# Mixture-of-experts kernel: gate and up as one product of 512 columns, the down projection as three float32r products, one accumulator, other weight rings

## The chip, the cores and the metric

The kernel runs on one core of a Trainium2 chip. The metric is the device time of one launch in microseconds (us). Five compute queues work side by side: TensorE (PE, matrix products; PEld is its weight loading), VectorE (DVE), ScalarE (ACT), GpSimd (POOL) and SyncE (SP, which here only issues transfers). Sixteen DMA engines move the data. Each queue runs its own instructions in order and waits on semaphores for the others.

## The reference

One block of a diffusion backbone: 512 tokens of width 1024 pass a token mixer (retention and gated delta rule) and then a mixture of experts. The change concerns the second half:

```
scores = sigmoid(xt @ w_router)                      # 512 tokens x 64 experts
sel    = 8 experts a token, from the best 4 of 8 groups
wts    = scores[sel] / sum * 2.5
yb     = (silu(xe @ w_gate[e]) * (xe @ w_up[e])) @ w_down[e]     # e = 0..63
routed = sum over the chosen experts of wts * yb
x      = x + g2 * rmsnorm(routed + shared) * norm_ffn_post
```

Each expert has w_gate and w_up of 1024x256 and w_down of 256x1024, all float32: 1 MB each, 3 MB an expert, 192 MB in all. The output must agree with a float32 computation.

## The kernel before, in words

The token mixer takes the first 700 us or so. Then phaseM walks over 64 experts, one block of 128 token slots for each, and a 65th block, "extra", for an expert with more than 128 tokens (its weights are fetched by an indirect load, L1191; a runtime loop at L1459 would handle further ones and runs zero times here).

For each expert e, in the loop at L1424:

- SP loads the three weight matrices into raw buffers (`load`, L1193). Gate and up share six buffers (`GU`), down has three (`DW`); a buffer is reloaded for expert e+3 as soon as it has been consumed.
- `convert` splits a gate or up matrix into two float32r matrices whose sum is the float32 value: ACT casts the high part (L1171, 2048 columns), DVE subtracts to get the low part (L1173). The down matrix stays float32.
- POOL gathers the 128 token rows (L1228); PE turns them (L1236), ACT and DVE split them into high and low (L1238, L1239).
- `proj` multiplies by gate and then by up. Each of 8 row blocks is three products, high x high, high x low, low x high (`mm3`, L111 to L113), 256 columns wide.
- `act` is silu(gate) times up (ACT L1248, DVE L1249), `turn_act` turns the result (L1256, L1258), and `down` multiplies by the float32 down matrix (L1267; four matrix products of 512 columns, each carried out in two passes, so eight instructions in the trace), scales the two halves (DVE L1271, ACT L1269) and adds the rows into a DRAM accumulator with an indirect DMA that adds (L1272, "the scatter").

There are two accumulators, `accd[0]` and `accd[1]`, used in turn (the last blocks all use 1). Scatters into the same accumulator wait for each other. After the loop both accumulators are read back (L1476), added (L1478), normalised (L1481 and the power on POOL at L127), scaled (L1484) and added to x (L1486, L1488).

The order of the instructions on each engine is set by a scheduler that takes the program's order and the dependencies; a buffer ring's depth therefore decides how far one queue runs ahead of another. On SP a load stands behind every load issued before it.

Of the kernel before, what the change touches and what calls it, by code (L numbers as in the profile page):

```python
# [19 lines left out]
D = 1024  # L20
# [3 lines left out]
NE = 64  # L24
# [47 lines left out]
class K:  # L72
# [128 lines left out]
    def run(self, upto="end"):  # L201
        nc, tc, a = self.nc, self.tc, self.a
        main = self.main = self.pool("main")
        self.pes = ExitStack()
        self.psum = self.pool("ps", es=self.pes, space=PSUM)
        self.wi = a["w_in"][0].rearrange("(k p) n -> p k n", p=128)
        self.ident = main.tile([128, 128], F32, name="ident")
        self.mhalf = main.tile([128, 1], F32, name="mhalf")
        nc.vector.memset(self.mhalf, -0.5)
        self.eps = main.tile([128, 1], F32, name="eps")  # L210
        nc.vector.memset(self.eps, EPS)
        self.vecT = main.tile([128, 68], F32, name="vecT")
# [3 lines left out]
        self.w8 = {"a": self.pool("w8a", bufs=4)}  # L216
# [768 lines left out]
    def phaseO(self):  # L985
# [7 lines left out]
        self.accd = [dp.tile([512, 1024], F32, name=f"acc{i}") for i in range(2)]  # L993
# [79 lines left out]
        def shared_down(t):  # L1073
            y = self.rawp.tile([128, 1024], F32, name="y", tag="raw")
            for c in range(2):
                ps = self.pa()
                for k in range(2):
                    nc.tensor.matmul(ps, sgs[t][:, k * 128:k * 128 + 128], wsh[2][:, k, c * 512:c * 512 + 512], start=k == 0, stop=k == 1)  # L1078
                nc.scalar.copy(y[:, c * 512:c * 512 + 512], ps)
            nc.scalar.dma_start(self.accd[0][t * 128:t * 128 + 128], y)  # L1080
# [77 lines left out]
    def phaseM(self):  # L1158
# [7 lines left out]
        T8 = lambda name: self.wt8([128, 2048], F32R, name, "b")  # L1166

        def conv(w, eng, n):
            h, l = T8("wh"), T8("wl")
            for i in range(0, 2048, max(n, 1024)):  # L1170
                nc.scalar.copy(h[:, i:i + max(n, 1024)], w[:, i:i + max(n, 1024)])  # L1171
            for i in range(0, 2048, n):
                eng(l[:, i:i + n], w[:, i:i + n], h[:, i:i + n].bitcast(F32), op=OP.subtract)  # L1173
            return h, l


        hx = self.hxpool.tile([128, 2, 2048], F32, name="wgu", tag="b0")
        GU = [self.wt8([128, 2048], F32, "w", "a") for _ in range(4)] + [hx[:, 0], hx[:, 1]]
        wd2 = q.tile([128, 2, 2048], F32, name="wd", bufs=1)
        DW = [wd2[:, 0], wd2[:, 1], self.keep.tile([128, 2048], F32, name="wd", tag="k0")]  # L1180
        NAMES3 = ("w_gate", "w_up", "w_down")
        wf = {n: a[n][0].rearrange("e (p k) f -> (e p) (k f)", p=128) for n in NAMES3}
        raw = lambda e, n: DW[e % 3] if n == 2 else GU[(2 * e + n) % 6]
# [11 lines left out]
        for e, n in ((0, 0), (0, 1), (1, 0), (0, 2), (1, 1), (2, 0), (1, 2), (2, 1), (2, 2)):  # L1195
            load(e, n)
# [22 lines left out]
        xg6, xg3 = q.tile([128, 3, 1088], F32, name="xg", bufs=1), self.hxpool.tile([128, 3, 1088], F32, name="xg", tag="b1")  # L1219
        xgs = [x[:, i] for x in (xg6, xg3) for i in range(3)]  # L1220
# [4 lines left out]
        def gather(ix):  # L1225
            xg = xgs[ng[0] % 6]
# [14 lines left out]
        def proj(out, x, w, first=True):  # L1241
            for k in range(8):
                s = slice(k * 256, k * 256 + 256)
                self.mm3(out, x[0][:, k], x[1][:, k], w[0][:, s], w[1][:, s], k == 0, k == 7)
# [7 lines left out]
        def turn_act(sg):  # L1252
# [4 lines left out]
            aT = q.tile([128, 256], F32, name="aT")  # L1257
            nc.scalar.copy(aT, ps[:, 0:256])  # L1258
            return aT

        def down(aT, sx, ws, wd, acc):
            y = self.rawp.tile([128, 1024], F32, name="y", tag="raw")
            for c in range(2):
                ps = self.pc()
                for k in range(2):
                    s, m = slice(k * 1024 + c * 512, k * 1024 + c * 512 + 512), slice(k * 128, k * 128 + 128)
                    nc.tensor.matmul(ps, aT[:, m], wd[:, s], start=k == 0, stop=k == 1)  # L1267
# [4 lines left out]
            nc.gpsimd.indirect_dma_start(self.accd[acc][:, :], bass.IndirectOffsetOnAxis(ap=sx, axis=0), y[:, :], None,  # L1272
                                         bounds_check=511, oob_is_err=False, compute_op=OP.add)

        cv = {}

        def convert(e, n):
            if e <= NE:
                cv[e, n] = conv(raw(e, n), tt, 2048)
                load(e + 3, n)  # L1280
# [3 lines left out]
        def prepare(e):  # L1284
# [8 lines left out]
            if e < NE:  # L1293
                W[e] = XG[e][:, 1024 + e:1025 + e]

        def make(e, part):
            if e > NE:
                return
            if part == 0:
                XT[e] = xtile()  # L1300
            turn(XT[e], part, XG[e])
# [4 lines left out]
        with tc.issue_after(self.scored.ins), tc.issue_after(listed.ins):  # L1306
# [3 lines left out]
            convert(1, 0)  # L1310
        for e in range(2):
# [103 lines left out]
        def extra_list(wi, px, colx):  # L1415
# [4 lines left out]
            slot_of(pv, 1, sl)  # L1420
            return wi, sl[1], sl[2]

        x = lambda e: [XT[e][:, h] for h in range(2)]
        for e in range(NE + 2):  # L1424
            if e == 3:
# [5 lines left out]
            if e <= NE:  # L1431
                pgu = self.pa()
                proj(pgu[:, 0:256], x(e), cv[e, 0])
# [13 lines left out]
            if e == NE - 2:  # L1447

                halves = lambda w: [w[:, i * 1024:i * 1024 + 1024] for i in range(2)]
                m0 = halves(raw(e, 0)) + halves(raw(e, 1))  # L1450
                x1 = halves(raw(e + 1, 0)) + halves(raw(e + 1, 1))
                for t in range(4):
                    nc.sync.dma_start(m0[t], self.accd[0][t * 128:t * 128 + 128])
                for t in range(2, 4):
                    nc.sync.dma_start(x1[t], self.out[t * 128:t * 128 + 128])


        cnt = nc.values_load(nx[0:1, 0:1], min_val=0, max_val=62)
        with tc.For_i(0, cnt) as _:  # L1459
            wi, ix, ws = extra_list(*extra_cols())  # L1460
            xT, xg = xtile(), gather(ix)
# [4 lines left out]
            w = [conv(raw(NE, n), tt, 1024) for n in range(2)]  # L1466
            pgu = self.pa()
            for n in range(2):
                proj(pgu[:, n * 256:n * 256 + 256], [xT[:, h] for h in range(2)], w[n])
            down(turn_act(act(pgu[:, 0:256], pgu[:, 256:512])), ix, ws, raw(NE, 2), 1)  # L1470


        m = halves(raw(NE, 0)) + halves(raw(NE, 1))
        r = q.tile([128, 4], F32, name="fr")
        for t in range(4):
            (nc.scalar if t % 2 else nc.sync).dma_start(m[t], self.accd[1][t * 128:t * 128 + 128])  # L1476
        for t in range(4):
            tt(m[t], m[t], m0[t], op=OP.add)  # L1478
            self.d("moe", m[t], t)
            junk = q.tile([128, 1024], BF, name="xT", bufs=2)  # L1480
            nc.scalar.activation(junk, m[t], AF.Square, accum_out=r[:, t:t + 1])  # L1481
            self.rsqrt(r[:, t:t + 1], r[:, t:t + 1], 1.0 / D, EPS)
        for t in range(4):
            nc.vector.scalar_tensor_tensor(m[t], m[t], r[:, t:t + 1], g2p, op0=OP.mult, op1=OP.mult)  # L1484
            if t < 2:
                nc.gpsimd.dma_start(self.out[t * 128:t * 128 + 128], m[t], accum_op=OP.add)  # L1486
            else:
                tt(m[t], m[t], x1[t], op=OP.add)  # L1488
                (nc.scalar if t % 2 else nc.sync).dma_start(self.out[t * 128:t * 128 + 128], m[t])
# [22 lines left out]
```

## Time and profile before

| | us |
|---|---|
| median of 3 runs (1405.65 to 1406.91) | 1406.16 |
| the profiled execution's own time | 1415.91 |
| its span in the trace | 1414.1 |
| mixer and router, until the first expert product | about 713 |
| PE busy over the span | 1324.8 (94%) |
| DVE, ACT, POOL busy | 906.7, 653.4, 409.6 |
| DMA read and written over the span | 326.59 MB and 48.31 MB |

The mean granted clock of TensorE is 0.971 of its full speed. Each busy time is a mean over stages with different limits, so the expert stage has to be read by itself. Matrix products overlap in the trace: the duration of one is not its cost, the distance between two starts is.

### The profile page before, as it was taken

What the parts mean: (1) busy time and instruction counts of PE and PEld (TensorE: products, weight loads), DVE (VectorE), ACT (ScalarE), POOL (GpSimd) and SP (SyncE); (2) the same over time, 40 slices, a digit from 0 to 9 for tenths busy, and PEclk for the clock granted to TensorE, in tenths of its full rate; (3) what the DMA queues carried; (4) which work ended last, traced back from release to release, by engine and by line L of the source; (5) the groups of instructions that cost most, each with busy time, mean ns of one, the idle gap of its engine ahead of it and who ended that gap; (6) DMA issues with size and microseconds to landing.
All of it is one profiled execution on the core that took longest, in us unless ns stands there. A gap on an engine that the chain in (4) does not pass through costs nothing.

```text
span 1414.1 us, 20716 instructions
## 1 busy us (share of the span) xinstructions
PE 1324.8 (94%) x7848; PEld 1074.7 (76%) x7848; DVE 906.7 (64%) x1270; ACT 653.4 (46%) x926; POOL 409.6 (29%) x330
## 2 busy tenths in 40 slices
PE   6999988899999999999999999999999999999990
PEld 1678866798787777778888787878788888878770
DVE  5645796457676555547668666666666666666543
ACT  5533432553333222334355555555656565555531
POOL 0315544865321000003222222222222222224312
PEclk9899998999999999999999999999999999999995
DMA  7554411102316577575699999999999999999954
GB/s 275 181 141 117 121 56 35 52 16 74 88 49 179 178 214 223 152 259 195 249 386 349 352 370 345 373 351 364 362 366 361 368 364 361 367 364 338 326 183 127
DMA packets 137817, 340.51 MB, mean 241 GB/s; under 512 B 28218, under 2 KB 83038, under 8 KB 112756
## 3 DMA queue, kind: packets, MB, share of 16 engines
q1 hardware_dynamic: 110952, 289.46, 57.2%
q0 software_dynamic: 19584, 38.99, 10.9%
q10 hardware_dynamic: 7180, 10.72, 2.2%
q8 instruction: 63, 1.03, 0.3%
q14 instruction: 38, 0.31, 0.1%
HBM read 326.59 MB, written 48.31 MB: 265 GB/s over the span
## 4 chain that ended last, share of the span: by engine, by line
PE 43%; DMA 7%; issue 1%; ACT 1%; POOL 1%; DVE 0%; DVEq 0%; SPq 0%; ACTq 0%; POOLq 0%
PE cs L1267 13%; PE acc L111 7%; PE acc L113 7%; PE acc L112 7%; DMA w<-in_w_up_dram 4%; PE ci L1236 3%; DMA w<-in_w_gate_dram 2%; PE ci L1066 2%; PE acc L1078 1%; PE acc L1256 1%; DMA w<-acc 1%; POOL fr L127 0%; DMA acc<-y,slots 0%; DMA acc<-y,sl_i 0%; ACT wh L1171 0%
## 5 line engine op out<-in xcount | busy, mean ns | idle before, releaser
L111 PE MATMUL acc<-wh,xT 128*128 128x256 f32 x1040 | 302.2, 291 | 0.0
L113 PE MATMUL acc<-wh,xT 128*128 128x256 f32 x1040 | 291.0, 280 | 0.0
L112 PE MATMUL acc<-wl,xT 128*128 128x256 f32 x1040 | 290.6, 279 | 0.0
L1173 DVE TENSOR_TENSOR wl<-w,wh 128x2048 fp32r<-128x2048 f32 x88 | 201.5, 2291 | 76.2 <-PE acc L112 75.2
L1267 PE MATMUL cs<-wd,aT 128*128 128x512 f32 x520 | 234.6, 594 | 4.5 <-DMA wd<-in_w_down_dram 3.6
L1272 POOL DMA_INDIRECT acc<-y,slots x64 | 101.9, 1593 | 466.5 <-ACT y L1269 427.8
L1171 ACT CAST wh<-w 128x2048 fp32r<-128x2048 f32 x88 | 167.5, 1904 | 99.5 <-PE acc L113 70.2
L111 PEld LDWEIGHTS acc<-wh,xT 128*128 128x128 f32 x1040 | 196.6, 189 | 0.2 <-issue 0.2
L112 PEld LDWEIGHTS acc<-wl,xT 128*128 128x128 f32 x1040 | 196.1, 189 | 0.2 <-issue 0.2
L113 PEld LDWEIGHTS acc<-wh,xT 128*128 128x128 f32 x1040 | 195.5, 188 | 0.0
L1267 PEld LDWEIGHTS cs<-wd,aT 128*128 128x128 f32 x520 | 93.8, 190 | 99.0 <-issue 95.1
L1239 DVE TENSOR_TENSOR xT<-ci,xT 128x512 fp32r<-128x512 f32 x130 | 89.2, 687 | 96.5 <-ACT xT L1238 96.1
L100 ACT CAST wu<-raw 128x1024 fp32r<-128x1024 f32 (+1 forms) x73 | 75.1, 1036 | 104.6 <-DMA raw<-in_w_in_dram 68.0
L111 PE MATMUL acc<-hTx,wu 128*128 128x512 f32 (+1 forms) x296 | 119.6, 404 | 1.5 <-ACT wu L100 1.5
L113 PE MATMUL acc<-hTx,wu 128*128 128x512 f32 (+1 forms) x296 | 117.7, 398 | 1.5 <-DVE wu L107 1.5
L1173 DVE TENSOR_TENSOR wl<-wgu,wh 128x2048 fp32r<-128x2048 f32 x42 | 96.2, 2291 | 34.6 <-PE acc L112 34.4
L112 PE MATMUL acc<-hLx,wu 128*128 128x512 f32 (+1 forms) x296 | 117.1, 396 | 0.0
L107 DVE TENSOR_TENSOR wu<-raw,wu 128x1024 fp32r<-128x1024 f32 (+1 forms) x61 | 78.7, 1299 | 55.4 <-ACT wu L100 55.4
L1171 ACT CAST wh<-wgu 128x2048 fp32r<-128x2048 f32 x42 | 79.8, 1901 | 53.5 <-PE acc L113 35.5
L1236 PEld LDWEIGHTS ci<-ident,xg 128*128 128x128 f32 x520 | 72.5, 191 | 30.6 <-issue 30.2
L1228 POOL DMA_INDIRECT xg<-h2d,slots x64 | 75.5, 1180 | 35.6 <-issue 18.0
L1236 PE MATMUL ci<-ident,xg 128*128 128x128 f32 x520 | 78.7, 275 | 0.1
(493 smaller groups left out, 2374.3 us busy)
## 6 DMA issues: line engine op xcount, KB each, us to landing
wd<-in_w_down_dram SPq DMA_DIRECT2D x64, 1024.0 KB
w<-in_w_gate_dram SPq DMA_DIRECT2D x43, 1024.0 KB
w<-in_w_up_dram SPq DMA_DIRECT2D x43, 1024.0 KB
raw<-in_w_in_dram SPq DMA_DIRECT2D x56, 512.0 KB
wgu<-in_w_gate_dram SPq DMA_DIRECT2D x21, 1024.0 KB
wgu<-in_w_up_dram SPq DMA_DIRECT2D x21, 1024.0 KB
mraw<-in_w_mod_dram SPq DMA_DIRECT2D x32, 512.0 KB
wm<-in_w_mod_dram SPq DMA_DIRECT2D x16, 512.0 KB
```

Of the source, the lines that this page charges most:

```text
L100: nc.scalar.copy(dst, src)
L107: (self.nc.gpsimd if eng == "pool" else self.nc.vector).tensor_tensor(dst, src, hi.bitcast(F32), op=OP.subtract)
L111: mm(out, ah, bh, start=start, stop=False)
L112: mm(out, ah, bl, start=False, stop=False)
L113: mm(out, al, bh, start=False, stop=stop)
L1171: nc.scalar.copy(h[:, i:i + max(n, 1024)], w[:, i:i + max(n, 1024)])
L1173: eng(l[:, i:i + n], w[:, i:i + n], h[:, i:i + n].bitcast(F32), op=OP.subtract)
L1228: nc.gpsimd.indirect_dma_start(xg[:, :], None, self.h2d[:, :], bass.IndirectOffsetOnAxis(ap=ix, axis=0), bounds_check=511, oob_is_err=False)
L1236: nc.tensor.transpose(ps[:, k * 128:k * 128 + 128], xv[:, :, c * 4 + k], self.ident)
L1239: tt(l, ps, h.bitcast(F32), op=OP.subtract)
L1267: nc.tensor.matmul(ps, aT[:, m], wd[:, s], start=k == 0, stop=k == 1)
L1272: nc.gpsimd.indirect_dma_start(self.accd[acc][:, :], bass.IndirectOffsetOnAxis(ap=sx, axis=0), y[:, :], None, bounds_check=511, oob_is_err ...
```

## The change: what it does

**One product for gate and up.** `proj` writes both into one 512-column product: a step reads the same 256 columns of the gate and the up matrix, which now lie in one tile (`GH`, `GL`, two experts deep). The eight row blocks are done as 0 to 3, then `turn_act`, then 4 to 7. ACT casts in halves of 1024 columns.

**Down in float32r.** The down matrix and the activations are split as well (`DP`, one buffer; `aT` gets a low part). A half of the result is six products of 512 columns (`down_half`). ACT casts both halves of the matrix, DVE subtracts for the first half, POOL for the second.

**Rings.** `DW` has two raw buffers instead of three, and a down buffer is reloaded for expert e+2 after its conversion instead of e+3 after its product. The gather has three buffers instead of six; a copy (`wcol`) of the slot weights frees them early.

**One accumulator.** `accd[1]` and the zeros written into it are gone. Expert 63 and the extra block are not scattered: `down_parts` leaves high and low parts of their rows in SBUF, and `finish` puts each row at its token with one-hot products (`place`), adds them to the accumulator's rows, and does the norm and the output in a written-out order. The accumulator's rows and x are read before that.

```diff
-        self.accd = [dp.tile([512, 1024], F32, name=f"acc{i}") for i in range(2)]
+        self.accd = dp.tile([512, 1024], F32, name="acc")
...
-        z = self.rawp.tile([128, 1024], F32, name="zero", tag="raw")
-        nc.gpsimd.memset(z, 0.0)
-        for t in range(4):
-            nc.scalar.dma_start(self.accd[1][t * 128:t * 128 + 128], z)
...
+        DW = [w2[:, 1], self.keep.tile([128, 2048], F32, name="wd", tag="k0")]
+        DP = self.hxpool.tile([128, 2, 2048], F32R, name="wdp", tag="b1")
...
+        def convert(e, n):
+            if e > NE:
+                return
+            w = raw(e, n)
+            if n < 2:
+                h, l = GH[e % 2][:, n], GL[e % 2][:, n]
+                for i in (0, 1024):
+                    nc.scalar.copy(h[:, i:i + 1024], w[:, i:i + 1024])
+                tt(l, w, h.bitcast(F32), op=OP.subtract)
+            else:
+                half = lambda x, c: x.rearrange("p (k f) -> p k f", k=2)[:, :, c * 512:c * 512 + 512]
+                for c, eng in enumerate((nc.vector, nc.gpsimd)):
+                    h = half(DP[:, 0], c)
+                    nc.scalar.copy(h, half(w, c))
+                    eng.tensor_tensor(half(DP[:, 1], c), half(w, c), h.bitcast(F32), op=OP.subtract)
+            load(e + (2 if n == 2 else 3), n)
...
+        def down_half(aT, c):
+            ps = self.pc()
+            for k in range(2):
+                s, m = slice(k * 1024 + c * 512, k * 1024 + c * 512 + 512), slice(k * 128, k * 128 + 128)
+                self.mm3(ps, aT[:, 0, m], aT[:, 1, m], DP[:, 0, s], DP[:, 1, s], k == 0, k == 1)
+            return ps
...
+            def place(t, j):
+                oh, y = blocks[j]
+                for c in range(2):
+                    if j == 0:
+                        PS[t, c] = self.pc() if t == 3 else self.pi() if c else self.pa()
+                    for i in range(2):
+                        nc.tensor.matmul(PS[t, c], oh[:, t], y[:, i * 1024 + c * 512:i * 1024 + c * 512 + 512],
+                                         start=j == 0 and i == 0, stop=j == len(blocks) - 1 and i == 1)
...
             if e <= NE:
                 pgu = self.pa()
-                proj(pgu[:, 0:256], x(e), cv[e, 0])
+                proj(pgu, x(e), e, range(4))
                 convert(e + 1, 1)
             if e > 0:
                 aT = turn_act(SG[e - 1])
             if e <= NE:
-                proj(pgu[:, 256:512], x(e), cv[e, 1])
+                proj(pgu, x(e), e, range(4, 8))
                 SG[e] = act(pgu[:, 0:256], pgu[:, 256:512])
                 convert(e + 2, 0)
             make(e + 2, 0)
+            if e > NE - 1:
+                Y.append(down_parts(aT, W[e - 1], GH[(NE - 1) % 2][:, len(Y)]))
+            elif e > 0:
+                down(aT, SL[e - 1], W[e - 1])
             if e > 0:
-                down(aT, SL[e - 1], W[e - 1], raw(e - 1, 2), 1 if e - 1 > NE - 4 else (e - 1) % 2)
-                load(e + 2, 2)
+                convert(e, 2)
             make(e + 2, 1)
             prepare(e + 4)
```

On PE, one expert's down projection and the start of the next gate product stand so before (`ci` is the turned token block, `cs` the down result, `acc` the gate and up result, `wd` the raw down matrix):

```order
L1236 MATMUL ci<-ident,xg 128x128 x3
L1267 MATMUL cs<-wd,aT 128x512 [waits DMAHW7_49,DVE_49,Activation_49]
L1267 MATMUL cs<-wd,aT 128x512 x3
L1236 MATMUL ci<-ident,xg 128x128 [waits DVE_49,PE_49]
L1236 MATMUL ci<-ident,xg 128x128 x3
L111 MATMUL acc<-wh,xT 128x256
L112 MATMUL acc<-wl,xT 128x256
```

and so after the change:

```order
L1249 MATMUL ci<-ident,xg 128x128 x3
L111 MATMUL cs<-wdp,aT 128x512 [waits Activation_49]
L112 MATMUL cs<-wdp,aT 128x512 [waits DVE_49]
L113 MATMUL cs<-wdp,aT 128x512 [waits DVE_49]
L111 MATMUL cs<-wdp,aT 128x512
L112 MATMUL cs<-wdp,aT 128x512
L113 MATMUL cs<-wdp,aT 128x512
L111 MATMUL cs<-wdp,aT 128x512
L112 MATMUL cs<-wdp,aT 128x512 [waits Pool_49]
L113 MATMUL cs<-wdp,aT 128x512
```

The four float32 products have become twelve float32r products, with new waits on DVE and, for the second half, on POOL.

On POOL, in the steady part of the expert loop, before (the semaphores DMASW0 to 7 go round over POOL's DMAs, in order of issue):

```order
L1272 DMA acc_4918<-y,slots 512x1024 [waits DMASW3_49,DVE_49,Activation_49]
L1228 DMA xg<-h2d,slots 128x1088 [waits DMASW0_49,PE_49]
L1272 DMA acc_4919<-y,slots 512x1024 [waits DMASW5_49,DVE_49,Activation_49]
L1228 DMA xg<-h2d,slots 128x1088 [waits DMASW2_49,PE_49]
L1272 DMA acc_4918<-y,slots 512x1024 [waits DMASW7_49,DVE_49,Activation_49]
```

and after:

```order
L1292 DMA acc<-y,slots 512x1024 [waits DMASW2_49,DVE_49,Activation_49]
L1195 TENSOR_TENSOR wdp<-wd,wdp 128x2x512 [waits DMAHW3_49,PE_49,Activation_49]
L1241 DMA xg<-h2d,slots 128x1088 [waits DMASW7_49,DVE_49,PE_49]
L1292 DMA acc<-y,slots 512x1024 [waits DMASW4_49,DVE_49,Activation_49]
L1195 TENSOR_TENSOR wdp<-wq,wdp 128x2x512 [waits DMAHW6_49,Activation_49]
```

Before, DMASW7 in the last row is the semaphore of the first scatter shown, two scatters back; after, DMASW4 in the fourth row is that of the scatter in the first row, directly before it. The subtraction for the second half of the down matrix now stands behind the scatter in POOL's queue.

## Rows read from the trace of the kernel before

**Rows 1.** Busy time of each engine by stretch, with TensorE's clock and DMA share

```profile
core 0: us, PE busy (x) PEld busy (x) DVE busy (x) ACT busy (x) POOL busy (x), PEclk, DMA share, GB/s
690.00:700.00 10.00, 10.00 (x80) 9.04 (x79) 7.23 (x18) 4.64 (x5) 2.19 (x1) 1.00 0.90 351
800.00:840.00 40.00, 40.00 (x264) 32.82 (x263) 26.66 (x25) 23.19 (x29) 10.53 (x8) 1.00 1.01 372
1320.00:1360.00 40.00, 37.34 (x228) 29.20 (x229) 24.13 (x23) 21.00 (x25) 11.45 (x8) 1.00 0.69 220
```

**Rows 2.** Chain of waits, 980 to 1010 us: start, duration, what

```profile
982.00 3.44 PE cs L1267 x8
...
985.87 0.12 PE acc L111
...
988.69 0.25 PE acc L1256 x2
...
992.20 3.44 PE cs L1267 x8
```

**Rows 3.** Timeline of PE, products of 512 columns (the shared expert): start, duration

```profile
656.14 0.40 PE L111 MATMUL acc<-wu,mh 128*128 128x512 f32 x1
...
660.72 0.39 PE L113 MATMUL acc<-wu,ml 128*128 128x512 f32 x1
```

**Rows 4.** DMA over 720 to 1300 us, in 40 equal slices

```profile
GB/s 395 345 346 357 357 356 348 392 344 356 351 354 391 346 349 359 353 371 359 373 354 373 364 346 371 371 376 351 370 364 359 377 340 382 368 357 376 348 363 343
DMA packets 40711, 209.59 MB, mean 361 GB/s; under 512 B 11674, under 2 KB 11674, under 8 KB 18885
```

**Rows 5.** Timeline of POOL, the last scatters: start, duration, [idle before, releaser]

```profile
1359.26 1.58 POOL L1272 DMA_INDIRECT acc<-y,slots  x1 [0.31 <-issue]
1369.86 1.56 POOL L1272 DMA_INDIRECT acc<-y,slots  x1 [9.02 <-DMA acc<-y,slots]
1377.71 1.56 POOL L1272 DMA_INDIRECT acc<-y,slots  x1 [6.29 <-ACT aT L1258]
1383.19 1.56 POOL L1272 DMA_INDIRECT acc<-y,sl_i  x1 [3.92 <-DMA acc<-y,slots]
```

**Rows 6.** Groups of instructions, 800 to 1280 us: busy us, mean ns, idle before

```profile
L1171 ACT CAST wh<-w 128x2048 fp32r<-128x2048 f32 x62 | 117.9, 1902 | 63.5 <-PE acc L113 61.5 <-PE acc L112 2.1
...
L1239 DVE TENSOR_TENSOR xT<-ci,xT 128x512 fp32r<-128x512 f32 x94 | 64.5, 686 | 60.8 <-ACT xT L1238 60.8
...
L1271 DVE TENSOR_SCALAR y<-cs,xg 128x512 f32<-128x512 f32 x48 | 35.8, 745 | 0.0
...
L1249 DVE TENSOR_TENSOR sg<-sg,acc 128x256 f32<-128x256 f32 x48 | 19.9, 415 | 0.0
```

**Rows 7.** Cast of half size, line 100: min/median/max ns

```profile
L100 ACT CAST wu<-raw x73: 292/1048/1061, 47.8 to 628.8; 128x1024 fp32r<-128x1024 f32 x72, 128x128 fp32r<-128x128 f32 x1
```

**Rows 8.** Subtraction of half and quarter size, line 107: min/median/max ns

```profile
L107 DVE TENSOR_TENSOR wu<-raw,wu x61: 285/1226/2308, 49.6 to 629.9; 128x1024 fp32r<-128x1024 f32 x60, 128x128 fp32r<-128x128 f32 x1
L107 POOL TENSOR_TENSOR wu<-raw,wu x24: 1266/1475/2974, 111.3 to 229.5; 128x512 fp32r<-128x512 f32 x24
```

**Rows 9.** Timeline of POOL and DVE side by side, 207 to 211 us

```profile
207.01 2.93 POOL L107 TENSOR_TENSOR wu<-raw,wu 128x512 fp32r<-128x512 f32 x2 [0.48 <-ACT wu L100]
207.11 1.71 DVE L573 TENSOR_TENSOR W<-W,tmp 96x504 f32<-96x504 f32 x1
...
210.50 0.67 DVE L573 TENSOR_TENSOR W<-W,tmp 96x494 f32<-96x494 f32 x1
```

**Rows 10.** Chain of waits, 1290 us to the end

```profile
1319.03 29.25 DMA w<-in_w_up_dram
...
1405.00 1.28 DVE w L1484
```

**Rows 11.** Timeline, the last down projection and the last output

```profile
1377.76 3.70 PE L1267 MATMUL cs<-wd,aT 128*128 128x512 f32 x8 [0.82 <-ACT aT L1258]
...
1408.58 0.34 ACTq L1489 DMA_DIRECT2D out_dram<-w  x1
```

More of the change, by code (lines that the diff above doesn't have):

```diff
@@ L1165, in phaseM @@
         xtile = lambda: q.tile([128, 2, 8, 128], F32R, name="xT", bufs=2)
[L1166 to L1174, printed above, removed]
+        self.w8s.close()
@@ L1177, in phaseM @@
+        self.w8as.close()
+        wp = self.pool("wM", reuse=True)
+        one = lambda name: wp.tile([128, 2048], F32, name=name)
+        GU = [one(f"wgu{i}") for i in range(3)]
+        GH, GL = [[wp.tile([128, 2, 2048], F32R, name=f"g{x}{i}") for i in range(2)] for x in "hl"]
+        w2 = q.tile([128, 2, 2048], F32, name="wq", bufs=1)
+        GU.append(w2[:, 0])
         hx = self.hxpool.tile([128, 2, 2048], F32, name="wgu", tag="b0")
-        GU = [self.wt8([128, 2048], F32, "w", "a") for _ in range(4)] + [hx[:, 0], hx[:, 1]]
@@ L1218, in phaseM @@
         listed = ts(slots, ps[:, 0:64], -1.0, 512.0, op0=OP.mult, op1=OP.add)
-        xg6, xg3 = q.tile([128, 3, 1088], F32, name="xg", bufs=1), self.hxpool.tile([128, 3, 1088], F32, name="xg", tag="b1")
-        xgs = [x[:, i] for x in (xg6, xg3) for i in range(3)]
+        xg3 = q.tile([128, 3, 1088], F32, name="xg", bufs=1)
+        xgs = [xg3[:, i] for i in range(3)]
         for x in xgs:
@@ L1239, in turn, with proj @@
             tt(l, ps, h.bitcast(F32), op=OP.subtract)
-        def proj(out, x, w, first=True):
-            for k in range(8):
+        def proj(out, x, e, ks=range(8)):
+            o = out.rearrange("p (n f) -> p n f", n=2)
+            for k in ks:
                 s = slice(k * 256, k * 256 + 256)
-                self.mm3(out, x[0][:, k], x[1][:, k], w[0][:, s], w[1][:, s], k == 0, k == 7)
+                self.mm3(o, x[0][:, k], x[1][:, k], GH[e % 2][:, :, s], GL[e % 2][:, :, s], k == 0, k == 7)
         def act(pg, pu):
@@ new lines, in places, with finish, then, add @@
+        def places(oh, row):
+            at = q.tile([128, 4], F32, name="at", bufs=2)
+            for t in range(4):
+                ts(at[:, t:t + 1], row, -128.0 * t, None, op0=OP.add)
+                ts(oh[:, t], cst("r0"), at[:, t:t + 1], None, op0=OP.is_equal)
+        def finish(m, x1, blocks):
+            mg = [x[:, 0:1024] for x in xgs] + [self.rawp.tile([128, 1024], F32, name="mg", tag="raw")]
+            r = q.tile([128, 4], F32, name="fr")
+            PS = {}
+            def place(t, j):
+                oh, y = blocks[j]
+                for c in range(2):
+                    if j == 0:
[3 more added lines that the diff above has]
+                                         start=j == 0 and i == 0, stop=j == len(blocks) - 1 and i == 1)
+            for t in (0, 1):
+                place(t, 0)
+            for t in range(4):
+                if t > 1:
+                    place(t, 0)
+                for j in range(1, len(blocks)):
+                    place(t, j)
+            last = [None]
+            def then(f):
+                if last[0] is None:
+                    last[0] = f()
+                else:
+                    with tc.issue_after(last[0].ins):
+                        last[0] = f()
+            def add(t):
+                for c in range(2):
+                    s = slice(c * 512, c * 512 + 512)
+                    then(lambda: tt(m[t][:, s], PS[t, c], m[t][:, s], op=OP.add))
+                self.d("moe", m[t], t)
+                junk = q.tile([128, 1024], BF, name="xT", bufs=2)
+                nc.scalar.activation(junk, m[t], AF.Square, scale=D ** -0.5, accum_out=r[:, t:t + 1])
+                nc.scalar.activation(r[:, t:t + 1], r[:, t:t + 1], AF.Identity, bias=self.eps)
+                if t == 1:
+                    nc.gpsimd.tensor_tensor(mg[t], m[t], g2p, op=OP.mult)
+                nc.gpsimd.tensor_tensor(r[:, t:t + 1], r[:, t:t + 1], self.mhalf, op=OP.pow)
+            def scaled(t):
+                then(lambda: tt(mg[t], m[t], g2p, op=OP.mult))
+            def out(t, s, eng):
+                then(lambda: nc.vector.scalar_tensor_tensor(mg[t][:, s], mg[t][:, s], r[:, t:t + 1], x1[t][:, s], op0=OP.mult, op1=OP.add))
+                eng.dma_start(self.out[t * 128:t * 128 + 128, s], mg[t][:, s])
+            whole = slice(0, 1024)
+            add(0)
+            scaled(0)
+            add(1)
+            out(0, whole, nc.sync)
+            add(2)
+            scaled(2)
+            add(3)
+            out(1, whole, nc.scalar)
+            scaled(3)
+            out(2, whole, nc.sync)
+            out(3, slice(0, 512), nc.scalar)
+            out(3, slice(512, 1024), nc.sync)
@@ L1310, in phaseM @@
             convert(1, 0)
+            convert(0, 2)
         for e in range(2):
@@ L1420, in extra_list @@
             slot_of(pv, 1, sl)
+            self.xrow = sl[0]
             return wi, sl[1], sl[2]
         x = lambda e: [XT[e][:, h] for h in range(2)]
+        halves = lambda e: [raw(e, n)[:, i * 1024:i * 1024 + 1024] for n in range(2) for i in range(2)]
+        Y = []
         for e in range(NE + 2):
+            if e == NE:
+                OH = GL[(NE - 1) % 2][:, 0, 0:1024].rearrange("p (b t n) -> p b t n", b=2, t=4)
+                OH = [OH[:, 0], OH[:, 1]]
+                row = q.tile([128, 1], F32, name="row", bufs=1)
+                nc.vector.tensor_copy(row, slots[:, NE - 1:NE])
+                places(OH[0], row)
+                places(OH[1], self.xrow)
             if e == 3:
@@ L1465, in phaseM @@
                 load(NE, n, wi)
-            w = [conv(raw(NE, n), tt, 1024) for n in range(2)]
+                convert(NE, n)
             pgu = self.pa()
[L1468 to L1489, printed above, removed]
+            proj(pgu, [xT[:, h] for h in range(2)], NE)
+            aT = turn_act(act(pgu[:, 0:256], pgu[:, 256:512]))
+            y = down_parts(aT, ws, GH[(NE - 1) % 2][:, 0])
+            finish(m, x1, [(OH[0], y)])
         self.pes.close()
```

59 lines of the change are left out of this document (32 added, 27 removed).

## The prediction, made before the changed kernel ran

> **What bounds the kernel now.** I read the busy time by stretch first. In the expert stage PE is busy 40.00 of 40 us at full clock, and in the same stretch the DMA engines are busy with a share of 1.01 [rows 1]. So two resources look full at once, and the question is which of them would go faster if the other were relieved. The chain of waits in the middle of the stage is PE alone: a down projection starts at 982.00 and the next at 992.20, a period of 10.2 us for an expert [rows 2]. That says PE is the last to finish; it does not say how far behind it the DMA is.
>
> The DMA view answers that. From 720 to 1300 us it moves 209.59 MB, 361 GB/s, and its 40 slices, 14.5 us each, lie between 340 and 395 GB/s [rows 4]. An expert at this mean takes 361 x 10.2 = 3.68 MB: 3 MB (3.15 million bytes) of weights, the rest gather and scatter. The loads are issued up to three experts ahead, so a DMA faster than PE would run dry now and then, and its share would fall below 1. It does not. At the end this shows: the last load on the chain, an up matrix, is issued at 1319.03 and lands 29.25 us later, PE is down to 37.34 of 40 and the DMA share is already falling [rows 1, 10]. One matrix is 1/3 of an expert's bytes, some 3.4 us at the mean rate; a landing of 29.25 us is a queue almost three experts long. I therefore take the DMA as the second bound, within about 1% of PE.
>
> **PE.** Gate and up were 48 products of 256 columns; 24 of them take 988.69 - 985.87 = 2.82 us, so 0.1175 us each and 5.64 us an expert [rows 2]. Now they are 24 products of 512. Twenty such steps took 660.72 - 656.14 = 4.58 us, 0.229 us each [rows 3]: 5.50 us. Down was 3.44 us [rows 2] and is 12 x 0.229 = 2.75 us. PE's work on an expert falls by 0.14 + 0.69 = 0.83 us, to about 9.4 us. Over the 62 experts of the steady stretch that would be 51 us, if nothing else held the period.
>
> **ACT, DVE, POOL.** Busy time an expert before is the stretch's, times 10.2/40: ACT 5.91, DVE 6.80, POOL 2.69 us [rows 1]. ACT loses two casts of 1.90 [rows 6] and gains six of 1.05 [rows 7]: 8.4 us. DVE gains a subtraction of 1024 columns, 1.23 us [rows 8], and one for `aT`, priced as the 0.415 us of line 1249 with its 256 columns [rows 6]: 8.4 us. POOL gains the other half of the down matrix, two times 1.48 us [rows 8]: 5.6 us. Alone, all three stay below PE's 9.4 us and are hidden by it, and by the DMA. They are not alone: beside a POOL subtraction of 2.93 us a DVE one takes 1.71 us where it takes 0.67 us once POOL has stopped [rows 9], so in those 2.93 us DVE does the work of some 1.15 and loses 1.8. If 0.69 us of this falls on the next `xT` subtraction, whose one input lies in PSUM, the loss is some 1.3 us, and DVE needs 9.7 us. That is below 10.2, with little left for waits.
>
> The Trainium skill speaks against this split: "SBUF — State Buffer", section "SBUF: two separate sides", calls the port pair that DVE and GpSimd share an exclusive lock, held for the whole instruction, when DVE reads two inputs from SBUF. By it DVE would stand still through the whole of POOL's subtraction; the time of that is the last of the rivals. The trace agrees only in part: both were slowed and neither stood still [rows 9].
>
> **The scatter.** With one accumulator each scatter waits for the landing of the one before. Before, this is seen only at the end, where the last blocks all go to accumulator 1. There the second scatter starts 1369.86 - 1359.26 = 10.60 us after the first and POOL sat idle for 9.02 us of it; a later pair, with the DMA emptier, is 5.48 us apart [rows 5]. So the price is a distance between 5.5 us (no load traffic) and 10.6 us (full traffic), the latter above 10.2. Behind the scatter in POOL's queue now stand the down matrix's second half and a gather, so PE's next down projection waits as well. It can't run far above the DMA's own pace, though: if the scatter stretches the period, fewer loads are issued, the queues empty, and the scatter lands sooner. I take 10.3 us, near the DMA's row, with 10.6 as one end and 9.75 as the other (the rate of the best slice nearly reached, 3.68 MB / 378 GB/s). Sum for the steady stretch: 62 x 0.1 = +6 us; ends 62 x 0.4 = +25 and 62 x -0.45 = -28.
>
> The shorter down ring has a price only here too: a down buffer is reloaded after a conversion that waits for POOL, and for one expert less ahead. With a landing near 29 us at the end it would be late; it is early enough if the queue is short. I leave it in the upper end.
>
> **Start.** The four zero writes are 2 MB that compete with the first loads: at the 351 GB/s of that stretch [rows 1], 6 us of DMA time. PE is busy there, and the first expert can't start before its tokens are gathered. The first conversions move, and one DVE subtraction now stands inside the list of slots, 2.3 us. I take -3 us, between -6 and +3.
>
> **Tail.** Before, from the end of the last down projection (1377.76 + 3.70 = 1381.46) to the span's end there are 32.6 us [rows 11]: two scatters in turn, the accumulator read back, sums, norm. After, behind the last down: two row parts (0.69 for ACT, as DVE's line 1239, and 0.745), 1.4 us; the first placing, four products of 0.229, 0.9 us; then DVE's written-out order: eight additions of 512 columns from PSUM at 0.69 [rows 6], three products of 1024 columns and three outputs at 1.28 each [rows 10], two half outputs at 0.745 [rows 6]: 14.7 us; and from the last output's issue to the end, 1414.1 - 1408.58 = 5.5 us [rows 11]. Together 22.5 us: -10 us (between -4, if the power on POOL is waited for twice, and -13). Against it the last blocks: their conversions and placings lie where only the extra block's short down projection was: +3 us (0 to +8).
>
> **Sum.** +6 - 3 - 10 + 3 = -4 us, 1411.9 us against the profiled execution's own 1415.91 (its span 1414.1 and 1.8 us around it). That execution was 9.75 us longer than the median of the runs, 1406.16; the same difference gives 1402 us.
>
> **The rivals.**
> - *The period falls with PE.* The DMA share of 1 would then only say that loads are always waiting, and the engines would serve them faster when asked. For it: slices up to 395 GB/s [rows 4]. Against it: PE asked for more than it got at the end, and 29.25 us of landing remained. At 9.75 us the steady stretch is -28 instead of +6: 1368 us. At PE's 9.4 us it would be 1346.
> - *The one accumulator sets the period (slower).* A scatter every 10.6 us, as at 1369.86, all the way: +25 instead of +6, 1421 us. It decides from the point at which a landing plus the wake-up of POOL exceeds the DMA's 10.2 us; for it speaks that the 10.60 us were measured with less load traffic than in the steady stretch. In the trace POOL's wait would read as that of a scatter for a scatter.
> - *DVE becomes the bound (slower).* DVE's 9.7 us, with the waits for ACT that it has now, line 1239 alone 60.8 us in 47 experts, 1.3 us each [rows 6], make 11.0 us if none overlaps POOL's work, 9.7 if all do. Half way, 10.4 with a jitter that hits the single converted down buffer, 10.7: 62 x 0.5 = +31 instead of +6, 1427 us. The worst form of it is that DVE stands still for all of POOL's 2.95 us: 8.4 + 2.95 = 11.4 us an expert, 62 x 1.1 = +68 on the forecast, 1470 us; chance 0.03, since the rows show both moving [rows 9]. (This is the skill's exclusive lock, above.)
>
> On the skill's figures for DMA: "Perfetto Trace Analysis", section "Engine Utilization", gives 358 GB/s as a core's share of memory bandwidth when its neighbour is active and about 435 GB/s as the ceiling of 16 engines for a core alone. This trace held 361 [rows 4]; by the ceiling an expert would take 8.5 us and the first rival would hold, by the share 10.3.
>
> **How the numbers follow.** A difference below 0.2% (2.8 us) can't be told from none by a measurement of this kernel. The DMA's pace as summed, 1402 with its own range 1392 to 1411: 0.42. The period falls with PE: 0.24. The single accumulator: 0.20. DVE: 0.14, the 0.03 among them. The forecast's own -4 is near the bound, so its 0.42 go 0.23 to faster, 0.13 to same, 0.06 to slower; of the slower rivals 0.03 end within 0.2% because the tail pays for them. Faster 0.47, same 0.16, slower 0.37. The range, 1370 to 1430, leaves out the lower part of the first rival and the worst of the last two.
>
> **What would show it.** Right: DMA share 1.0 and 10.2 to 10.4 us between down projections in the middle; PE busy 36 to 37 of 40 us, waiting for `wdp` (POOL or DVE) or for a load; POOL's scatter waiting for a scatter; about 22 us from the last down projection to the end. Wrong: a period under 10 us with more than 375 GB/s (first rival); a period of 10.6 or more with a DMA share below 0.97 and POOL idle before line 1292 (second); DVE busy in nearly all of a period, its subtractions well above 2.3 us (third); or PE's clock falling where it now has gaps, which no row of the expert stage before lets me price.

## The result, and the profile after

The changed kernel took 1479.98 us (median of 5 runs, 1479.46 to 1483.85) against 1406.16 us: a ratio of 1.0517, 95% interval 1.0488 to 1.0546. I had forecast 1402 us and a range up to 1430. It is slower by 74 us.

The profiled execution spans 1477.9 us, 63.8 more than before; the rest of the 74 is that the execution profiled before was 9.75 us above its median. Most of that lies ahead of the experts: its first gather starts at 697.81 us, in the four runs of its loop below, each with a small edit, at 687.4 to 692.3. The 63.8 us split by the scatters on POOL's timeline, first and 63rd:

| | first scatter | 63rd scatter | period between | 63rd to the end |
|---|---|---|---|---|
| before | 730.85 | 1369.86 | 10.31 | 44.2 |
| after | 739.25 | 1440.31 | 11.31 | 37.6 |
| difference | +8.4 | | 62 x 1.0 = +62.1 | -6.7 |

So the expert loop carries the loss. The 11.31 us are a mean: from the 11th period to the 48th nearly every one is 11.37 to 11.39 us, against 10.20 before; the first ten take 12.02 (10.26 before), for a reason that stays open, and the last fourteen some 10.6. The same view as [rows 1], in the middle of the loop:

```profile
core 0: us, PE busy (x) PEld busy (x) DVE busy (x) ACT busy (x) POOL busy (x), PEclk, DMA share, GB/s
1000.00:1040.00 40.00, 33.38 (x161) 26.74 (x160) 40.00 (x33) 28.77 (x39) 15.88 (x10) 1.00 0.95 312
1200.00:1240.00 40.00, 34.84 (x167) 28.09 (x165) 40.00 (x30) 28.39 (x40) 20.17 (x12) 1.00 0.97 340
```

Before, the column with 40.00 was PE's; now it is DVE's. PE has gaps, the clock holds, and the DMA is no longer full. The timeline of DVE shows one whole period, from one long subtraction (`gl`, the low part of a gate or up matrix) to the next:

```profile
996.88 5.54 DVE L1189 TENSOR_TENSOR gl<-wq,gh 128x2048 fp32r<-128x2048 f32 x1
1002.34 0.41 DVE L1274 TENSOR_TENSOR aT<-acc,aT 128x256 fp32r<-128x256 f32 x1
1002.68 0.14 DVE L1397 COPY wcol<-xg 128x1 f32<-128x1 f32 x1
1002.74 0.41 DVE L1264 TENSOR_TENSOR sg<-sg,acc 128x256 f32<-128x256 f32 x1
1003.07 2.28 DVE L1189 TENSOR_TENSOR gl<-wgu,gh 128x2048 fp32r<-128x2048 f32 x1
1005.27 0.68 DVE L1252 TENSOR_TENSOR xT<-ci,xT 128x512 fp32r<-128x512 f32 x1
1005.87 0.73 DVE L1291 TENSOR_SCALAR y<-cs,wcol 128x512 f32<-128x512 f32 x1
1006.53 1.21 DVE L1195 TENSOR_TENSOR wdp<-wq,wdp 128x1024 fp32r<-128x1024 f32 x1
1007.66 0.68 DVE L1252 TENSOR_TENSOR xT<-ci,xT 128x512 fp32r<-128x512 f32 x1
1008.26 5.53 DVE L1189 TENSOR_TENSOR gl<-wgu,gh 128x2048 fp32r<-128x2048 f32 x1
```

The period is 1008.26 - 996.88 = 11.38 us without a pause. The same 2048-column subtraction takes 2.28 us for the gate matrix and 5.54 us for the up matrix. What differs is on POOL's timeline: its half of the down matrix runs inside the long one, and right behind the scatter.

```profile
996.09 1.74 POOL L1292 DMA_INDIRECT acc<-y,slots  x1 [0.30 <-issue]
997.31 2.95 POOL L1195 TENSOR_TENSOR wdp<-wd,wdp 128x1024 fp32r<-128x1024 f32 x1
```

5.54 - 2.28 = 3.26 us for 2.95 us of POOL: the VectorE instruction loses all of POOL's time and a little more. It ends at 1002.42, 2.16 us after POOL's end at 1000.26, and alone it needs 2.28: so it did hardly anything until POOL was done, though its recorded start is 0.43 us ahead of POOL's. In this trace that holds for each of the 55 times that a POOL subtraction makes a VectorE one longer: the VectorE one ends 2.15 to 2.17 us after POOL's. POOL can be the one that waits, too. Four times near the end its recorded start comes 1.03 to 1.08 us after VectorE's; VectorE then takes 2.28 to 2.34 us, and POOL 3.5 instead of 2.95:

```profile
1344.47 2.34 DVE L1189 TENSOR_TENSOR gl<-wgu,gh 128x2048 fp32r<-128x2048 f32 x1
1345.55 3.52 POOL L1195 TENSOR_TENSOR wdp<-wq,wdp 128x1024 fp32r<-128x1024 f32 x1
```

PE is made to wait: its third down product stands for DVE, which has just come out of the long subtraction (the release is named `wcol`; the low part of `aT` ends just before it).

```profile
1002.81 0.50 PE L113 MATMUL cs<-wdp,aT 128*128 128x512 f32 x1 [1.66 <-DVE wcol L1397]
```

### The profile page after: what moved, and what is told of

Its sections match the earlier page's. It is cut to its first block, busy times and chain, and to the rows that moved or that the text cites. A ratio compares the mean times of both kernels' runs of the same rounds, so it can differ in the third digit from the quotient of the medians.

```text
span 1477.9 us, 18576 instructions
## 1 busy us (share of the span) xinstructions
PE 1303.6 (88%) x6580; PEld 1054.0 (71%) x6580; DVE 1164.6 (79%) x1485; ACT 796.2 (54%) x1192; POOL 576.9 (39%) x388
## 5 line engine op out<-in xcount | busy, mean ns | idle before, releaser
L1189 DVE TENSOR_TENSOR gl<-wgu,gh 128x2048 fp32r<-128x2048 f32 x108 | 360.2, 3336 | 8.1 <-ACT gh L1188 8.1
L1188 ACT CAST gh<-wgu 128x1024 fp32r<-128x1024 f32 x216 | 225.7, 1049 | 57.8 <-PE acc L113 56.8
L111 PE MATMUL acc<-gh,xT 128*128 128x512 f32 x520 | 215.8, 415 | 0.0
L113 PE MATMUL acc<-gh,xT 128*128 128x512 f32 x520 | 205.3, 395 | 0.0
L112 PE MATMUL acc<-gl,xT 128*128 128x512 f32 x520 | 203.2, 391 | 0.0
L113 PE MATMUL cs<-wdp,aT 128*128 128x512 f32 x260 | 109.1, 423 | 81.4 <-DVE wcol L1397 68.0
L112 PE MATMUL cs<-wdp,aT 128*128 128x512 f32 x260 | 105.4, 405 | 14.7 <-POOL wdp L1195 14.7
L113 PEld LDWEIGHTS acc<-gh,xT 128*128 128x128 f32 x520 | 97.9, 188 | 22.8
L112 PEld LDWEIGHTS acc<-gl,xT 128*128 128x128 f32 x520 | 98.5, 190 | 17.0
L111 PEld LDWEIGHTS acc<-gh,xT 128*128 128x128 f32 x520 | 98.7, 190 | 16.0
L111 PE MATMUL cs<-wdp,aT 128*128 128x512 f32 x260 | 109.0, 419 | 0.2 <-ACT aT L1273 0.2
L1195 POOL TENSOR_TENSOR wdp<-wq,wdp 128x1024 fp32r<-128x1024 f32 x33 | 97.4, 2953 | 5.4 <-ACT wdp L1194 5.4
L1189 DVE TENSOR_TENSOR gl<-wq,gh 128x2048 fp32r<-128x2048 f32 x22 | 99.1, 4505 | 0.3 <-ACT gh L1188 0.3
L1195 POOL TENSOR_TENSOR wdp<-wd,wdp 128x1024 fp32r<-128x1024 f32 x32 | 94.9, 2965 | 7.7 <-ACT wdp L1194 7.7
```

What stands on the lines that cost most here:

```text
L111: mm(out, ah, bh, start=start, stop=False)
L112: mm(out, ah, bl, start=False, stop=False)
L113: mm(out, al, bh, start=False, stop=stop)
L1188: nc.scalar.copy(h[:, i:i + 1024], w[:, i:i + 1024])
L1189: tt(l, w, h.bitcast(F32), op=OP.subtract)
L1195: eng.tensor_tensor(half(DP[:, 1], c), half(w, c), h.bitcast(F32), op=OP.subtract)
```

## The experiments

The theories: (1) POOL's subtraction stops DVE's and so sets the period; (2) the one accumulator sets it; (3) the shorter down ring does. The periods below are from the 1st to the 63rd scatter, over 62.

**Take each cost away, alone and together.** The first run has both halves on DVE (`for c, eng in enumerate((nc.vector, nc.vector))`). The second alternates between two accumulators, of which the second is neither zeroed nor added, so half of the experts are missing from the output (an excerpt of the edit):

```diff
-                down(aT, SL[e - 1], W[e - 1])
+                down(aT, SL[e - 1], W[e - 1], self.accd2 if e % 2 else self.accd)
```

> The changed kernel with both halves of the down matrix's subtraction on VectorE, none on GpSimd. Theory 1 (the GpSimd subtraction stops VectorE's, which takes 5.53 us beside it and 2.28 alone): VectorE needs 8.12 + 1.21 = 9.33 us an expert instead of 11.37, the period falls to that of TensorE and the DMA, 10.2 to 10.4 us, 1480 - 62 x 1.0 = 1417 us (1408 to 1425). Theory 2 (the single accumulator sets the period): no change, 1475 to 1485. Theory 3 (the shorter down ring does): no change either, or some us slower, since VectorE now frees the buffer later.

> The changed kernel with scatters that alternate between two accumulators again; the second one is neither zeroed nor added to the output, so half of the experts are missing from it. Theory 1: 1475 to 1485, the period stays 11.37 us. Theory 2: a period of 10.2 to 10.4 us, 1410 to 1425. Theory 3: as theory 1.

The third run has both edits.

> Both edits of the runs before together (the second accumulator again not in the output). Theory 1: 1405 to 1420; what it is below the run with the subtractions on VectorE alone is the price of the one accumulator once VectorE no longer sets the period, 0 to 25 us by the prediction's bounds. Theory 2: as the run with two accumulators alone. Theory 3: 1475 to 1485.

The fourth prices the accumulator in the kernel before, by a constant 1 as the accumulator's number in `down`.

> The kernel before with every scatter into accumulator 1 (accumulator 0 still holds the shared expert and is still added). It prices the one accumulator by itself. If a scatter takes the 10.6 us of the rows at the end all the way: 1406 + 62 x 0.4 = 1431 us. If it lands within the 10.2 us of the period: 1404 to 1410.

| kernel | median us | ratio to before (95%) | period |
|---|---|---|---|
| changed | 1479.98 | 1.0517 (1.0488 to 1.0546) | 11.31 |
| both halves on DVE | 1456.70 | 1.0350 (1.0297 to 1.0403) | 11.03 |
| two accumulators | 1473.86 | 1.0476 (1.0441 to 1.0511) | 11.23 |
| both edits | 1412.06 | 1.0025 (1.0005 to 1.0044) | 10.25 |
| before, one accumulator | 1434.98 | 1.0177 (1.0121 to 1.0233) | 10.74 |

Theory 1 expected 1417 for the first and got 1457: it is right about what binds, and it missed that the next limit stands close behind. DVE's subtraction is back at 2.29 us there, but POOL's scatters are 11.17, 12.06 and 11.41 us apart, as the timeline of that run shows. Where an engine is named, its part of `y` was long done (the whole `y` at 1007.90 us for the scatter at 1012.43), and the wait is for the landing of the scatter before: 10.6 us from issue, the median of 43 in that run's DMA view. TensorE's clock is not the reason: the granted one was 0.99 of full speed over 1000 to 1040 us, where these distances stand, and fell only later (0.92 over 1200 to 1240):

```profile
1001.26 2.22 POOL L1292 DMA_INDIRECT acc<-y,slots  x1 [6.12 <-ACT gh L1188]
...
1012.43 1.93 POOL L1292 DMA_INDIRECT acc<-y,slots  x1 [6.49 <-DMA acc<-y,slots]
...
1024.49 1.59 POOL L1292 DMA_INDIRECT acc<-y,slots  x1 [7.68 <-DVE gl L1189]
...
1035.90 2.93 POOL L1292 DMA_INDIRECT acc<-y,slots  x1 [7.66 <-ACT xT L1251]
```

The two limits do not add up, the longer one counts: taking away the scatter's alone gives 6 us, the subtraction's alone 23, both together 68. The accumulator alone costs the kernel before 27 us (1434.98 - 1408.4, its runs beside it), the forecast's rival said 25. Theory 3 falls as the cause of the 74 us: both edits bring the time back with the short ring in place. (ScalarE waits there for down loads, 61.4 us over 800 to 1280 us; that is where the DMA's lateness now shows. A run with the deeper ring was not made.)

The second run shows one thing more. Between 1288 and 1347 us POOL's subtraction starts 1.03 us after VectorE's seven times in a row and is the one that waits (3.5 us), and the seven periods there are 9.46 to 9.85 us, with PE busy 60.00 of 60 us over 1290 to 1350 (the next period is 14.12). So it is not the split as such that holds the period at 11.38 us, but the order in which the two meet.

**What in POOL's instruction stops DVE.** In the kernel with two accumulators POOL's subtraction is replaced: in one run by a memset to zero, which reads nothing, in the next by the high half times zero, which reads one input. The low half that POOL writes is zero in both, so the down product lacks it.

> The changed kernel with two accumulators (1473.9 us as it was), and on GpSimd a memset of the 1024 columns in place of the subtraction: it writes the same bytes and reads nothing; the low half is zero, so the down product lacks it. Theory P (VectorE stands still because GpSimd reads SBUF through a port that both need): VectorE's 2048-column subtraction goes back to 2.3 us, its busy time an expert to 8.1 us, and the time falls to the DMA's, 1405 to 1420. Theory Q (any GpSimd work beside it, or the writes, slow VectorE): the subtraction stays above 4 us and the time above 1450.

> As the run with the memset, but GpSimd multiplies the high half by zero: one input read from SBUF instead of two, the same bytes written (the low half is zero again). Theory P in the form that only two inputs need the shared port: 1405 to 1420, VectorE's subtraction near 2.3 us. Theory P in the form that any read does: VectorE loses what the GpSimd instruction lasts, 1 to 3 us, and the time is 1420 to 1475.

The memset gave 1415.17 us, with DVE's subtraction at 2286 ns mean and DVE no longer full. It mostly ran at another place, but the three times that it lay wholly within a subtraction, that took no longer than alone (1.22 us for this size):

```profile
1374.74 1.23 DVE L1199 TENSOR_TENSOR wdp<-wd,wdp 128x1024 fp32r<-128x1024 f32 x1
```

```profile
1374.92 0.95 POOL L1197 MEMSET wdp<- 128x1024 f32 x1 [2.41 <-PE cs L112]
```

The one-input instruction gave 1422.46 us, and lies just where the subtraction did:

```profile
1003.71 4.18 DVE L1190 TENSOR_TENSOR gl<-wgu,gh 128x2048 fp32r<-128x2048 f32 x1
```

```profile
1004.14 1.61 POOL L1197 TENSOR_SCALAR wdp<-wdp 128x1024 fp32r<-128x1024 f32 x1
```

4.18 - 2.28 = 1.90 us lost for 1.61 us of POOL. One input read from SBUF is enough, and the loss goes with POOL's duration; again VectorE ends 2.14 us after POOL. The Trainium skill, "SBUF — State Buffer", section "SBUF: two separate sides", says that GpSimd and a VectorE instruction with two SBUF inputs lock a shared port pair for a whole instruction, whichever starts first, if the GpSimd one reads SBUF. These two runs agree with it, the memset with no loss and the multiplication with a full one. On who goes first the recorded starts do not bear it out: where VectorE is 0.4 us ahead by them, it is VectorE that waits.

> The kernel before with one subtraction of 1024 columns an expert added on GpSimd, in two pieces of 512, whose result is not used. Theory P: VectorE's subtractions that meet it take 2.9 us longer, its busy time goes from 6.8 to some 9.8 us an expert, still under 10.2, and the time rises only by what VectorE's order of work delays, 1406 to 1425. If the price of GpSimd's subtraction were one of DMA or TensorE, VectorE's durations would stay at 2.29 us.

```diff
                 cv[e, n] = conv(raw(e, n), tt, 2048)
+                if n == 1 and e > 1:
...
+                    for i in (0, 512):
+                        nc.gpsimd.tensor_tensor(dm, raw(e, n)[:, i:i + 512], cv[e, n][0][:, i:i + 512].bitcast(F32), op=OP.subtract)
```

1411.25 us, ratio 1.0014 (0.9994 to 1.0035): no difference. The longer subtractions that I expected came only seven times, at the start and the end of the loop (3.19 us at 714.39, 4.52 at 1320.44). In the steady part the work fell beside other DVE instructions, those that read one input from PSUM:

```profile
1004.65 2.63 POOL L1284 TENSOR_TENSOR dummy<-w,wh 128x512 f32<-128x512 f32 x2 [4.47 <-issue]
```

```profile
1004.48 0.41 DVE L1249 TENSOR_TENSOR sg<-sg,acc 128x256 f32<-128x256 f32 x1
1004.81 0.74 DVE L1271 TENSOR_SCALAR y<-cs,xg 128x512 f32<-128x512 f32 x1
1005.47 0.68 DVE L1239 TENSOR_TENSOR xT<-ci,xT 128x512 fp32r<-128x512 f32 x1
```

They take what they always do [rows 6]: 0.41, 0.74 and 0.68 us. So not POOL's work as such costs DVE, but what it meets there.

**Where PE's saving went.** With both costs gone the loop is still at 10.25 us, though PE needs less. Half of each down load is left out from expert 3 on, `t[:, 0:1024]`; first in the changed kernel with both edits and the copies on ScalarE (below), then in the kernel before.

> The changed kernel with both subtractions on VectorE, two accumulators and the copies on ScalarE (1408.6 us as it was), with only half of each down matrix loaded from expert 3 on (0.5 MB less an expert, the rest of the buffer is stale). If the DMA sets its period of 10.25 us: the period falls to VectorE's and TensorE's 9.25 to 9.5, the time to 1350 to 1365. If TensorE or VectorE sets it: 1400 to 1409.

> The kernel before with the same halved down loads. If TensorE sets its 10.2 us with the DMA just behind: the steady stretch stays, only the late loads at the end go, 1390 to 1402. If the DMA were the first bound: 1350 to 1370.

The first went from 1408.58 to 1362.33 us, the second to 1404.54, ratio 0.9973 (0.9958 to 0.9987). In the first the period became 9.52 us (9.43 in the steady part), and PE is full again where, with whole loads (the second row), it was not:

```profile
1200.00:1240.00 40.00, 40.00 (x196) 33.60 (x196) 39.84 (x43) 34.19 (x48) 12.09 (x9) 1.00 0.99 336
```

```profile
1200.00:1240.00 40.00, 35.36 (x165) 28.20 (x164) 32.75 (x37) 27.98 (x39) 11.56 (x8) 1.00 0.98 351
```

The kernel before kept its 10.20 us; it gained less than the 1390 to 1402 us that I expected. PE's saving is real, and over the whole loop the loads hide it: with whole loads the run with both edits moved 360 GB/s over 720 to 1300 us, the kernel before 361 [rows 4]. DVE, with both subtractions, stands at 39.84 of 40 us in the first row, so which of the two sets 9.43 is not shown. Nor does the DMA's share tell that it binds: it is 0.99 at 336 GB/s there and 0.98 at 351 with whole loads.

The 10.25 us are a mean as well. In the run with both edits the scatters of the 11th to the 20th period come every 9.65 us, with 375 GB/s over 840 to 940 us, and those of the 51st to the 60th every 10.89, with 340 GB/s over 1240 to 1340. So the saving does show until the loads fall behind. Why their rate falls over the loop is open.

**The late start.** In the changed kernel the first product comes 25.1 us after the first gather (720.53 and 695.38), before 15.1 us; this distance is 14.9 to 15.5 us in all profiled runs of the loop before, and 25.1 to 26.2 in those of the changed one that leave DVE's queue there as it is. So the start costs some 10 us, more than the 8.4 of the first scatter. DVE's queue has the copies of the first slot weights, which wait for gathered rows, ahead of a product of the shared expert and of `xT`'s low parts. I moved them to ScalarE (`nc.scalar.copy if e < 4`), then back to DVE behind that product (`with tc.issue_after(self.shg.ins)`).

> The run with VectorE's subtractions and two accumulators (1412.1 us), with the copies of the slot weights of experts 0 to 3 on ScalarE instead of VectorE. In the changed kernel VectorE waits 11.3 us there for gathered rows, with a product behind it for which TensorE waits 7.3 us. If that is the late start (the first scatter comes 8.4 us later than before): 1403 to 1407. If the late loads are: 1410 to 1414.

> The changed kernel with both subtractions on VectorE and two accumulators (1412.1 us as it was), the copies of the first slot weights kept on VectorE but placed behind the shared expert's last product. The run with these copies on ScalarE only moved the wait: there ScalarE waited 12.3 us for the gathered rows with the shared expert's silu behind it. If the queue order is the late start: the first product comes some 15 us after the first gather as before, not 25, and the time falls by 8 to 10 us to 1402 to 1404. If the late first loads are: the distance stays at 25 us and the time at 1409 to 1414.

1408.58 and 1406.32 us, both between the times expected of the two causes. The distance was 26.1 us with both edits alone, 25.3 with the copies on ScalarE, and 22.5 with them later on DVE. On ScalarE the wait only changed its queue, 12.33 us with the silu behind it. In the second run the copies still stand ahead of the low parts:

```profile
710.40 0.15 DVE L1399 COPY wcol<-xg 128x1 f32<-128x1 f32 x1 [4.04 <-DMA xg<-h2d,slots]
```

So the queue order accounts for 3 to 4 of the 10 us by this run; the rest is open, the late first loads among what was not tried.

**Versions that might beat both.** The kernel before with only the changed kernel's end; and the changed kernel without its costs and with nothing left out (second accumulator zeroed in four writes, read back, added).

> The kernel before, loop unchanged (two accumulators, float32 down, three down buffers), with the changed kernel's end: expert 63 and the extra block placed by one-hot products, the accumulators read ahead and added, the written-out order of the norm. In the changed kernel the time from the scatter of expert 62 to the end is 37.5 us against 44.3 before. If that carries over: 1408 - 5 to - 9, 1399 to 1403, faster than both kernels. If the end waits for the last loads of the DMA anyway: 1406 to 1410.

> The same with the second accumulator zeroed, read back and added, so that nothing is left out: the changed kernel without its three costs. The zeros are 2 MB of DMA (6 us, partly hidden), the additions 4 x 1.22 us on VectorE, partly hidden: 1404 to 1412 if the late start is gone, against 1408 for the kernel before; a clear gain over it is not expected, since the DMA holds both at 10.2 us.

1409.92 us, ratio 1.0008 (0.9989 to 1.0027), and 1414.21 us, ratio 1.0044 (1.0028 to 1.0061). Neither does. The end, 37.6 us after the 63rd scatter in the changed kernel, was 42.7 in the first, where DVE waits 5.06 us for the accumulators' rows and adds them; its scatters came every 10.27 us in the steady part, 10.20 before. In the second the end was 46.8 us, so with a second accumulator to read back the new end gains nothing, and the time missed the 1404 to 1412 us expected.

## Why the prediction was wrong

**The step that failed is DVE's price beside POOL.** The prediction put DVE's work at 8.4 us an expert (measured alone: 11.38 - 3.26 = 8.12) and the loss beside POOL at 1.3 us; it is 3.26. I read [rows 9] as a rate: DVE "does the work of some 1.15" in 2.93 us of POOL, and took from it that neither engine stood still. But those were two POOL instructions beside two short DVE ones, that at 207.11 in the rows and this one, from the same timeline of DVE:

```profile
208.85 1.61 DVE L572 TENSOR_TENSOR tmp<-N,W 96x494 f32<-96x494 f32 x1
```

Each lost about 1 us, in the size of one POOL instruction (1.27 us at least [rows 8]). That fits turns by whole instructions as well as a shared rate; a single long POOL instruction beside a single long DVE one leaves no such turns, and in the changed kernel DVE ended 2.16 us after it, having done next to nothing beside it. I named this as the last rival, DVE standing still through all of POOL's time, 1470 us, and gave it 3 in 100. Its mechanism is what happened. That its period, 11.4 us, is the 11.38 measured is partly luck: it added 8.4 and 2.95 where 8.12 and 3.26 were measured. Its 1470 us miss the measured 1480 by about what the start had wrong.

**The scatter was second, and undersized.** I took 10.3 us as its period with 10.6 as the upper end, arguing that a scatter that stretches the period empties the queues and then lands sooner. With DVE relieved it held 11.03 us, with a DMA share of 0.91 to 0.98 in three stretches of 40 us after 1000 us. Its scatters took 10.6 us to land, at 338 GB/s over 720 to 1300 us, less traffic than the 361 of the kernel before. At this traffic the argument of the emptying queues did not hold; in the changed kernel, at 324 GB/s over 760 to 1420 us, the landing takes 7.6 us. The scatter's price was hidden in the result by DVE's 11.38. The two costs put the steady stretch at +62 us where the sum had +6.

**PE and DMA were right on the mean.** With the down loads halved the loop ran at 9.52 us, where PE's work had been put at 9.4; with whole loads and without the two costs it ran at 10.25. That is an average of a faster first part, as the first rival had it, and a slower last one. The sum's +6 compared 10.3 with one period of 10.2; the mean period before was itself 10.31, since its 51st to 60th take 11.02 each. Without the two costs the kernel stands at 1406 to 1414 us, against the forecast's 1402.

**Start and end.** The start was -3 and came to +8.4, some +10 from the first gather on. I had seen one subtraction moved into the slot list, not the copies that wait for a DMA; these explain 3 to 4 us of it, the rest is open. The end was -10 + 3 = -7, and came to -6.7; from the last down product's end, 1453.60, to the end there are 24.3 us, 22.5 forecast.

## What to carry to other kernels

Work that is moved to GpSimd to relieve VectorE is best placed beside VectorE instructions that read PSUM; here, beside a subtraction of two SBUF inputs, one of the two engines stood still, and mostly it was VectorE, which lost 3.26 us where the move had spared it 1.2. Where they must meet, look at which one waits: in this kernel, with POOL's start about 1 us after VectorE's, POOL lost 0.6 us and VectorE nothing. When an engine's saving is to count, first ask what is full beside it: here the DMA was, over the loop, within 1% of TensorE, so that 0.8 us an expert saved on TensorE was worth next to nothing, while VectorE's period of 11.4 us cost 62 us. And of limits that lie close together, taking away one shows the next, so try them alone and together.

## What the runs showed of the hardware that was not expected

- By the recorded starts VectorE's instruction was under way when POOL's began (996.88 and 997.31), yet it ended 2.16 us after POOL's, with 2.28 us of work of its own: a recorded start does not show that an instruction is moving. GpSimd's spans are rough, so the order of the starts is not certain. In the changed kernel POOL waited instead (3.5 us) where its start was 1.03 us behind.
- A multiplication by zero with one SBUF input on POOL stops VectorE as well (1.90 us for 1.61).
- A scatter that must wait for the one before comes every 11.0 us on average with 0.91 to 0.98 of the DMA busy (landing 10.6 us), more than the 10.6 us at the end of the kernel before; in the kernel before with one accumulator it was 10.74. What sets the difference is open.
- The DMA's busy share reads 0.99 at 336 GB/s and 1.01 at 375 GB/s in runs of this case: a share near 1 alone did not tell its pace.
